# Three pairs of rounded weight tiles instead of two in a streaming-encoder block on one core

## The chip, the core and the metric

The kernel runs on one core of a Trainium2 chip. The core has a matrix engine (TensorE, PE in the profile, with its weight loads as PEld), a vector engine (DVE), a scalar engine (ACT), GpSimd (POOL) and a sync engine (SP) that here issues most DMAs. The metric is the device time of one execution in microseconds (us). The time before is the median of three runs.

## The reference

One layer of a hybrid encoder block on 256 tokens of width 2048, all in float32, and the result must be close to float32. Four sublayers follow each other, each ending in a layer norm over the residual stream:

```python
h = LN(alpha*h + 0.5*swiglu(h, ffn1))            # 2048 -> 2 x 5504 -> 2048
proj = h @ w_in                                   # q/k/v of A, latents of B, two gates
y_a = chunked_attention(q, k, v, rel_bias) @ w_o_a     # 16 heads of 64
y_b = latent_attention(q_lat, kv_lat, ...) @ w_o_b     # 16 heads, rotary part of 64
h = LN(alpha*h + (sig(g_a)*y_a + sig(g_b)*y_b) @ w_out)
h = LN(alpha*h + cross_attention(h, LN(mem)))     # 4 heads of 512, 256 memory tokens
h = LN(alpha*h + 0.5*swiglu(h, ffn2))
```

About 480 MB of weights are read once. Each weight meets all 256 tokens.

## The kernel before

**Split operands.** A float32 product is made of three faster products. Each operand is rounded to a shorter format (float32r), hi, and what the rounding leaves out, lo, is kept as a second operand of that format; hi·hi, hi·lo and lo·hi are added in PSUM. For weights this is done by `halves` (lines 257 to 266): two casts on ACT of 128x1024 each (line 262) write hi, then one subtraction on DVE (line 265) writes lo. Activations go the same way through `split` (lines 253 and 254).

**Weights as a queue.** The block's work is a list of items. An item is a function that issues matmuls and the weight pieces it needs, 1 MB each, 128x2048 elements. `run` (lines 177 to 242) walks the list. Before an item's function is called, it loads its pieces and, as far as `ahead` allows, those of later items: `fetch` starts the DMA on SP into one of three raw tiles, `halves` issues the roundings into a pair of tiles from `unit` (pools whi and wlo, `UNITS` each). What limits the look-ahead is the last line:

```python
def ahead(need, held):
    if nxt < need:
        return True
    n = sum(not early(w) for w in queue[need:nxt])
    return (nxt < need + 5 and (early(queue[nxt]) or n < 2)
            and held + live + slots(queue[nxt]) <= UNITS)
```

`live` counts pieces loaded but not used up, `held` the pairs that an item keeps for a later one. With `UNITS` at 2 there is the piece in use and one more.

**Two sorts of step.** In `pair_group` (lines 643 to 667) a group makes two output blocks for both halves of the tokens from eight steps of two k-tiles each. A plain step (`mm_pair`, line 309) takes 24 matmuls. At steps 2, 4 and 6 a scheme of the Strassen kind (`mm_sums`, line 363) does with 21. It needs sums of weight blocks, made on DVE by `weight_sums` (lines 246 and 248) in a stage tile (H5 in most groups, a raw tile in others), rounded by `halves` into X2 (hi) and X3 (lo), which have one buffer each. It also needs sums of activations (`sum_forms`, lines 319 to 328), some of which stay in four tiles of 128x256 from `w1` for all groups of a stage. After step 6, `shared` (lines 674 to 679) takes four PSUM banks out; these are the banks in which the next group begins, half a dozen matmuls after step 7.

**Other users of the small tiles.** `total` (lines 279 to 288) adds two halves of a PSUM tile through a `w1` tile; the attention heads' queries and keys stay there until their scores are made.

**Order.** The program is written in the order of the items, but a scheduler orders each engine's instructions by priority (`prio`) and by its own estimate of when each can run, and picks free tiles of a pool. Each engine then works in that order and waits at the first instruction that isn't ready. Transposes of activations are DMAs on SP, issued behind the last weight load (`issue_after`), so loads and transposes share one ordered queue. POOL issues a few loads of biases, norm vectors, memory tokens and rotary swaps; their descriptors are written into a scratch of the SBUF whose size the program's builder sets (`kernel`, line 1761).

Of the kernel before, what the change touches and what calls it, by code (L numbers as in the profile page):

```python
# [47 lines left out]
RMS_EPS = 1e-6  # L48
NEG = -1e30
MAGIC = 0x5F3759DF  # L50
UNITS = 2
SOON, NEAR, LATE = 400, 100, -400
WARM = 9
HEADS = ("H4", "H5", "X2", "X3")
# [45 lines left out]
class Kernel:  # L100
    def __init__(self, ctx, tc, t, out):
        self.tc, self.nc, self.t, self.out = tc, tc.nc, t, out

        def pool(name, bufs=1, **kw):
            return ctx.enter_context(tc.tile_pool(name=name, bufs=bufs, **kw))

        self.const = pool("const")
        self.wraw = pool("wraw", 3)
        self.whi = pool("whi", UNITS)
        self.wlo = pool("wlo", UNITS)  # L110
        self.blocks = pool("blocks")
# [22 lines left out]
        return self.work.tile(list(shape), dt, tag="w2", bufs=6, name=self.name("w2"))  # L134

    def w1(self, shape=(P, S), dt=F32):
        return self.work.tile(list(shape), dt, tag="w1", bufs=6, name=self.name("w1"))

    def sm(self, tag, n, dt=F32, bufs=None):
        return self.small.tile([P, n], dt, tag=tag, name=self.name(tag), **({"bufs": bufs} if bufs else {}))  # L140
# [36 lines left out]
    def run(self):  # L177
# [3 lines left out]
        def slots(w):  # L181
            return 0 if isinstance(w, tuple) and w[1] else 1
# [35 lines left out]
        def early(w):  # L218
            return not isinstance(w, Sums) and w[1] is not None and "early" in w[1]
# [8 lines that stand above are left out]
# [1543 lines left out]
```

## Time and profile before

| | us |
|---|---|
| median of three runs | 2436.41 |
| lowest, highest | 2433.37, 2439.05 |
| span of the profiled execution | 2432.9 |
| PE busy in the span | 2423.0 |
| DVE busy | 2121.1 |
| ACT busy | 1551.3 |

The span reaches from the first to the last instruction of one execution. For the profiled execution itself the page gives no time beside this span, so the three timed runs, 0.5 to 6.2 us longer, show what lies around it. In the rows, "mm" and "at" are PSUM tiles, "hi" and "lo" a weight pair, "T", "H" and "X" blocks of activations or, where line 262 or 265 writes X from H, rounded weight sums. A row of the timeline has its start, its length, the engine, the line and the operation, the tiles and the count of merged instructions, and in brackets the engine's idle time before it and what ended it.

### The profile page before, as it was taken

How to read it: one execution, taken by the hardware profiler on the slowest of the kernel's cores; microseconds unless marked ns; L12 is line 12 of the kernel's file. 1: busy time of each engine (PE TensorE's matmuls, PEld its weight loads, DVE VectorE, ACT ScalarE, POOL GpSimd, SP SyncE). 2: the span in 40 equal slices, each digit the busy share in tenths (PEclk: the TensorE clock that was granted, in tenths of full speed). 3: DMA queues.
4: the chain of work that ended last, by engine and by line, in shares of the span. 5: the costliest groups of instructions: out<-in, count | busy, mean ns of one | idle time of the engine just before them, and what ended most of it. 6: DMA issues, size and time to landing. Idle time of an engine off the chain costs nothing.

```text
span 2432.9 us, 29701 instructions
## 1 busy us (share of the span) xinstructions
PE 2423.0 (100%) x11286; PEld 2022.5 (83%) x11286; DVE 2121.1 (87%) x2423; ACT 1551.3 (64%) x2017; POOL 36.1 (1%) x81
## 2 busy tenths in 40 slices
PE   9999999999999999999999999999999999999999
PEld 8888888889888888888888888888888888888887
DVE  8999989899878898789788889979879999888997
ACT  6676745666555557878565687765666675556762
POOL 0000000000000001000000000000000000000000
PEclk9999999999999999999999999999999999999999
DMA  7766656666645657776577577655556666666665
GB/s 268 252 214 213 208 199 221 212 199 222 225 172 209 208 209 248 230 209 175 184 249 251 167 236 218 219 184 189 190 199 214 229 221 210 216 208 205 201 223 182
DMA packets 176414, 516.20 MB, mean 212 GB/s; under 512 B 111728, under 2 KB 112496, under 8 KB 121104
## 3 DMA queue, kind: packets, MB, share of 16 engines
q1 hardware_dynamic: 170816, 495.83, 61.2%
q0 software_dynamic: 4592, 17.30, 2.2%
q8 instruction: 88, 1.44, 0.2%
q10 hardware_dynamic: 864, 1.18, 0.1%
q14 instruction: 54, 0.44, 0.1%
HBM read 485.30 MB, written 2.10 MB: 200 GB/s over the span
## 4 chain that ended last, share of the span: by engine, by line
PE 90%; DVE 4%; ACT 3%; DMA 1%; issue 1%; SPq 0%; DVEq 0%; ACTq 0%
PE at L309 24%; PE mm L309 23%; PE mm L296 11%; PE at L363 10%; PE mm L363 10%; PE mm L275 5%; PE mm L277 2%; DVE lo L265 2%; ACT hi L262 1%; PE at L1028 1%; DMA raw<-w_xq 0%; PE at L1499 0%; PE at L1082 0%; PE at L275 0%; DMA raw<-w_o_b 0%
## 5 line engine op out<-in xcount | busy, mean ns | idle before, releaser
L262 ACT CAST hi<-raw 128x1024 fp32r<-128x1024 f32 (+1 forms) x852 | 805.3, 982 | 454.2 <-PE at L309 155.0
L265 DVE TENSOR_TENSOR lo<-raw,hi 128x2048 fp32r<-128x2048 f32 (+1 forms) x427 | 902.3, 2114 | 139.3 <-ACT hi L262 133.4
L309 PE MATMUL mm<-hi,T 128*128 128x512 f32 (+1 forms) x1328 | 311.1, 384 | 1.3 <-DVE v L397 1.3
L309 PEld LDWEIGHTS mm<-hi,T 128*128 128x128 f32 x1328 | 247.3, 188 | 48.5 <-DVE v L397 1.8
L309 PE MATMUL at<-hi,T 128*128 128x512 f32 x1152 | 275.5, 389 | 0.0
L262 ACT CAST X<-H 128x1024 fp32r<-128x1024 f32 (+1 forms) x166 | 170.6, 1034 | 162.0 <-DVE H L246 128.1
L309 PEld LDWEIGHTS at<-hi,T 128*128 128x128 f32 x1152 | 216.2, 188 | 45.1
L265 DVE TENSOR_TENSOR X<-H,X 128x2048 fp32r<-128x2048 f32 (+1 forms) x83 | 186.7, 2250 | 68.6 <-ACT X L262 68.6
L309 PE MATMUL mm<-lo,T 128*128 128x512 f32 (+1 forms) x664 | 160.4, 382 | 0.0
L309 PEld LDWEIGHTS mm<-lo,T 128*128 128x128 f32 x664 | 123.7, 188 | 22.8
L309 PE MATMUL at<-lo,T 128*128 128x512 f32 x576 | 142.4, 389 | 0.0
L309 PE MATMUL at<-hi,H 128*128 128x512 f32 x560 | 133.7, 389 | 0.0
L309 PEld LDWEIGHTS at<-lo,T 128*128 128x128 f32 x576 | 108.1, 188 | 22.5
L309 PEld LDWEIGHTS at<-hi,H 128*128 128x128 f32 x560 | 104.9, 188 | 21.6
L309 PE MATMUL mm<-hi,H 128*128 128x512 f32 x480 | 115.5, 391 | 0.3 <-DVE w L679 0.3
L248 DVE TENSOR_TENSOR H<-H,raw 128x512 f32<-128x512 f32 (+1 forms) x166 | 112.2, 676 | 2.2
L309 PEld LDWEIGHTS mm<-hi,H 128*128 128x128 f32 x480 | 89.5, 188 | 19.3 <-DVE w L679 0.8
L246 DVE TENSOR_TENSOR H<-raw 128x1024 f32<-128x1024 f32 (+1 forms) x83 | 99.4, 1198 | 0.9 <-DMA raw<-w_gate 0.8
L363 PE MATMUL mm<-X,X 128*128 128x512 f32 x342 | 91.1, 392 | 0.0
L262 ACT CAST X<-raw 128x1024 fp32r<-128x1024 f32 (+1 forms) x54 | 55.4, 1036 | 48.7 <-DVE raw L248 38.7
L363 PE MATMUL at<-X,X 128*128 128x512 f32 (+1 forms) x315 | 82.5, 386 | 0.9 <-DVE X L265 0.5
L849 ACT COPY w<-w 128x1024 uint16<-128x1024 uint16 (+1 forms) x60 | 75.8, 1276 | 0.6 <-DMA w<-w 0.5
(373 smaller groups left out, 4123.1 us busy)
## 6 DMA issues: line engine op xcount, KB each, us to landing
raw<-ffn_w_in SPq DMA_DIRECT2D x150, 1024.0 KB, 4.8
raw<-ffn_w_out SPq DMA_DIRECT2D x66, 1024.0 KB, 4.8
raw<-w_gate SPq DMA_DIRECT2D x32, 1024.0 KB, 4.8
raw<-ffn_w_out_r SPq DMA_DIRECT2D x16, 1024.0 KB, 4.9
raw<-w_qk SPq DMA_DIRECT2D x16, 1024.0 KB, 5.5
raw<-w_o_b SPq DMA_DIRECT2D x16, 1024.0 KB, 4.8
raw<-w_out SPq DMA_DIRECT2D x16, 1024.0 KB, 5.2
raw<-w_xk SPq DMA_DIRECT2D x16, 1024.0 KB, 5.3
```

The source lines that it names most:

```text
L246: self.nc.vector.tensor_tensor(two[0], two[1], raw[:, :m].unsqueeze(1).to_broadcast([P, 2, m]), ALU.add)
L248: self.nc.vector.tensor_tensor(t[:, a * m:a * m + m], t[:, b * m:b * m + m], raw[:, a * m:a * m + m], ALU.add)
L262: self.last_hi = self.nc.scalar.copy(hi[:, c:d], src[:, c:d])
L265: self.last_lo = self.nc.vector.tensor_tensor(lo[:, :n], src, hi[:, :n].bitcast(F32), ALU.subtract)
L275: self.nc.tensor.matmul(ps, hi[j], x.both(kt), start=(j == 0), stop=False)
L277: self.last_mm = self.nc.tensor.matmul(ps[:, :S], lo[j], x.at(0, kt), start=False, stop=(j == n - 1))
L296: self.last_mm = self.nc.tensor.matmul(ps, x.at(xi, kt)[:, tt * P:(tt + 1) * P], w[wi][:, j * 512 + c:j * 512 + c + m], start=(start and j ...
L309: self.last_mm = self.nc.tensor.matmul(ps[tt, g][:, :n], x.at(xi, kt)[:, tt * P:(tt + 1) * P], w[wi][:, c:c + n], start=first and j + wi + ...
L363: self.last_mm = self.nc.tensor.matmul(bank[:, :m], a[xi], v[wi][:, c * m:(c + 1) * m], start=own and first and wi + xi == 0, stop=own and ...
L849: self.nc.scalar.copy(self.words(u, n).rearrange("p (c k) -> p k c", k=2), self.words(s, n).rearrange("p (k c) -> p k c", k=2))
L1028: nc.tensor.matmul(ps[:, c0:c0 + nk], q[:, tt * P:(tt + 1) * P], k[:, :nk], start=(j == 0), stop=(j == len(parts) - 1))
```

## The change

The diff, whole:

```diff
-UNITS = 2
+UNITS = 3
 SOON, NEAR, LATE = 400, 100, -400
...
     def w1(self, shape=(P, S), dt=F32):
-        return self.work.tile(list(shape), dt, tag="w1", bufs=6, name=self.name("w1"))
+        return self.work.tile(list(shape), dt, tag="w1", bufs=4, name=self.name("w1"))
...
-    nc = bacc.Bacc("TRN2", target_bir_lowering=False, num_devices=1)
+    nc = bacc.Bacc("TRN2", target_bir_lowering=False, num_devices=1, dynamic_dma_scratch_size=2048)
```

There is a third tile of 8 KB per partition for hi and one for lo. Two small tiles of 1 KB each go, and the scratch for descriptors of POOL's DMAs is set to 2 KB. `ahead` now lets one more piece be loaded and rounded before an item, so its roundings are issued one weight earlier; what is computed stays. The program has the same instructions on every engine. Of PE's 11107 matmuls 514 stand at another place, of ACT's 1949 and DVE's 2425 instructions some 700 each, POOL's order is the same, and of SP's 580 some 40 stand elsewhere.

Two places show how. The first is the end of a gate group (the third `pair_group` of w_gate). On DVE, L265 lo is the rounding of a plain weight (lo_6070 before and lo_6046 after are the same weight, that of step 7), L265 X_908 is the rounding of the sums of step 6, L246 and L248 build sums in H5, and L676 to L679 are `shared`. Before:

```order
L248 TENSOR_TENSOR H_904_6008<-H_904_6008,raw_6006 128x512 x2
L265 TENSOR_TENSOR X_908_6039<-H_904_6008,X_907_6038 128x2048
L265 TENSOR_TENSOR lo_6070<-raw_6067,hi_6069 128x2048
L676 TENSOR_TENSOR w_917_6104<-w_915_6102,mm_5942 128x512
L265 TENSOR_TENSOR lo_6098<-raw_6095,hi_6097 128x2048
L677 TENSOR_TENSOR w_916_6103<-w_916_6103,w_917_6104 128x512
L678 TENSOR_TENSOR w_917_6104<-w_917_6104,mm_5943 128x512
L679 TENSOR_TENSOR w_918_6105<-w_916_6103,mm_5943 128x512
```

And now, in the same place on DVE:

```order
L248 TENSOR_TENSOR H_904_5984<-H_904_5984,raw_5982 128x512
L265 TENSOR_TENSOR lo_6046<-raw_6043,hi_6045 128x2048
L265 TENSOR_TENSOR X_908_6018<-H_904_5984,X_907_6017 128x2048
L265 TENSOR_TENSOR lo_6077<-raw_6074,hi_6076 128x2048
L246 TENSOR_TENSOR H_923_6121<-raw_6119 128x1024
L248 TENSOR_TENSOR H_923_6121<-H_923_6121,raw_6119 128x512
L265 TENSOR_TENSOR lo_6115<-raw_6112,hi_6114 128x2048
L676 TENSOR_TENSOR w_917_6104<-w_915_6102,mm_5952 128x512
L248 TENSOR_TENSOR H_923_6121<-H_923_6121,raw_6119 128x512
L677 TENSOR_TENSOR w_916_6103<-w_916_6103,w_917_6104 128x512
L678 TENSOR_TENSOR w_917_6104<-w_917_6104,mm_5953 128x512
L679 TENSOR_TENSOR w_918_6105<-w_916_6103,mm_5953 128x512
```

The lo of step 7 moved from behind X to ahead of it, and ahead of L676 there are now both lo of the next group's first two steps and most of the sums for its step 2. On ACT at the same place (X_907 is the hi of the sums, L674 and L675 are the copies of `shared`), before:

```order
L262 CAST X_907_6038<-H_904_6008 128x1024
L262 CAST hi_6069<-raw_6067 128x1024
L262 CAST X_907_6038<-H_904_6008 128x1024
L262 CAST hi_6069<-raw_6067 128x1024
L262 CAST hi_6097<-raw_6095 128x1024
L674 COPY w_915_6102<-mm_5940 128x512
L262 CAST hi_6097<-raw_6095 128x1024
L675 COPY w_916_6103<-mm_5941 128x512
```

and now:

```order
L262 CAST hi_6045<-raw_6043 128x1024 x2
L262 CAST X_907_6017<-H_904_5984 128x1024 x2
L262 CAST hi_6076<-raw_6074 128x1024 x2
L262 CAST hi_6114<-raw_6112 128x1024
L674 COPY w_915_6102<-mm_5950 128x512
L262 CAST hi_6114<-raw_6112 128x1024
L262 CAST X_927_6164<-H_923_6121 128x1024
L675 COPY w_916_6103<-mm_5951 128x512
```

Both casts of step 7's weight stand ahead of X's, and the casts of the next group's second weight and one of its step 2 sums stand ahead of L675. The second place is in the second query group of the cross attention, on DVE, where L323 and L254 make a form of activations (w, then T) for the sums step that reads it. Before:

```order
L248 TENSOR_TENSOR T_1892_12194<-T_1892_12194,raw_12192 128x512
L323 TENSOR_TENSOR w_1894_12201<-w_1893_12200,w_1894_12201 128x128
L323 TENSOR_TENSOR w_1894_12201<-w_1893_12200 128x128
L265 TENSOR_TENSOR lo_12231<-raw_12192,hi_12230 128x1536
L254 TENSOR_TENSOR T_1877_12114<-w_1894_12201,T_1877_12114 128x512
L265 TENSOR_TENSOR X_1898_12236<-T_1892_12194,X_1897_12235 128x2048
```

and now:

```order
L265 TENSOR_TENSOR lo_12164<-raw_12161,hi_12163 128x2048
L265 TENSOR_TENSOR X_1883_12130<-T_1876_12086,X_1882_12129 128x2048
L254 TENSOR_TENSOR T_1877_12114<-w_1894_12201,T_1877_12114 128x512
L246 TENSOR_TENSOR T_1892_12170<-raw_12168 128x1024
L265 TENSOR_TENSOR lo_12210<-raw_12168,hi_12209 128x1536
L248 TENSOR_TENSOR T_1892_12170<-T_1892_12170,raw_12168 128x512
```

The form's last row (L254, T_1877) moved ahead of the same step's L246 and lo (lo_12231 before, lo_12210 now).

## The prediction

> **What bounds the kernel now.** I read the page's head and the chain that ended last first, to see which engine carries the time.
>
> ```profile
> span 2432.9 us, 29701 instructions
> ...
> PE 2423.0 (100%) x11286; PEld 2022.5 (83%) x11286; DVE 2121.1 (87%) x2423; ACT 1551.3 (64%) x2017; POOL 36.1 (1%) x81
> ...
> PE 90%; DVE 4%; ACT 3%; DMA 1%; issue 1%; SPq 0%; DVEq 0%; ACTq 0%
> ```
>
> TensorE is busy for 2423.0 of 2432.9 us. A busy matmul row can hide a wait, because 0.39 us long matmuls overlap, so I counted matmuls in stretches of the span (columns: stretch, its length, then busy us and count of PE, PEld, DVE, ACT, POOL, then the granted clock and the DMA share).
>
> ```profile
> 200.00:300.00 100.00, 100.00 (x442) 82.59 (x441) 93.66 (x89) 69.28 (x79) 0.00 (x0) 1.00 0.63 202
> ...
> 1900.00:2000.00 100.00, 100.00 (x442) 82.47 (x441) 96.06 (x95) 69.41 (x80) 3.22 (x6) 1.00 0.67 218
> 2000.00:2100.00 100.00, 99.47 (x439) 82.00 (x438) 90.46 (x83) 58.48 (x65) 0.00 (x0) 1.00 0.60 204
> ```
>
> The granted clock is 1.00. 442 matmuls in 100 us are one per 0.227 us, and this pace is the same in distant stretches; where it stalls, some are missing (439: three matmuls, 0.7 us). So nearly all of the time is matmuls at their own pace, and the change, which leaves all 11107 matmuls of the program as they are, can only work on stalls. What they are is best read from the waits of PEld, the weight loads, since those don't overlap (us in total, times, longest).
>
> ```profile
> PEld mm L363 <- DVE X L265: 2.2, 8, 0.3
> PEld at L363 <- DVE X L265: 2.1, 5, 1.0
> PEld mm L309 <- DVE v L397: 1.8, 1, 1.8
> PEld at L363 <- ACT X L262: 1.5, 4, 0.5
> ...
> PEld mm L309 <- DVE w L679: 0.9, 2, 0.8
> PEld at L1082 <- ACT T L849: 0.9, 2, 0.6
> PEld mm L363 <- DVE T L254: 0.8, 1, 0.8
> ...
> PEld mm L363 <- DVE H L254: 0.7, 2, 0.3
> ...
> PEld at L1082 <- ACT H L849: 0.4, 1, 0.4
> PEld mm L275 <- ACT hi L262: 0.4, 1, 0.4
> ```
>
> Only the last row is a weight pair that came late, which is what the change gives a third of. The largest sum, 5.8 us in 17 stalls, is X: the rounded sums of weights (X2, X3), which have one buffer before and after, but are made by the same DVE and ACT queues. One such stall, in the gate groups:
>
> ```profile
> 827.83 1.29 PE L309 MATMUL mm<-hi,T 128*128 128x512 f32 x5
> 828.99 0.96 PE L363 MATMUL at<-X,X 128*128 128x512 f32 x3
> 829.79 0.40 PE L363 MATMUL mm<-X,T 128*128 128x512 f32 x1
> ...
> 828.99 0.53 PEld L363 LDWEIGHTS at<-X,X 128*128 128x128 f32 x3 [0.29 <-DVE X L265]
> ...
> 824.44 2.29 DVE L265 TENSOR_TENSOR lo<-raw,hi 128x2048 fp32r<-128x2048 f32 x1 [0.74 <-ACT hi L262]
> 826.65 2.28 DVE L265 TENSOR_TENSOR X<-H,X 128x2048 fp32r<-128x2048 f32 x1
> ```
>
> From 827.83 to 829.79 eight matmuls start in 1.96 us where 8 x 0.227 = 1.81 would do: 0.15 us are lost, 0.14 less than PEld's 0.29. I take 0.14 off each stall of the waits. X ended at 828.93 because DVE did a pair's lo (2.29 us) before it, and waited 0.74 us for ACT before that.
>
> **The change, part by part. The third pair.** The steady state of a group shows what it does. A plain step (24 matmuls) and a sums step (21) take turns, 45 x 0.227 = 10.20 us for both.
>
> ```profile
> 797.46 3.79 PE L309 MATMUL at<-hi,T 128*128 128x512 f32 x16
> 801.09 1.98 PE L309 MATMUL at<-lo,T 128*128 128x512 f32 x8
> ...
> 804.26 0.39 PE L363 MATMUL at<-lo,T 128*128 128x512 f32 x1
> ...
> 806.75 0.84 PE L363 MATMUL mm<-X,w 128*128 128x512 f32 x3
> ...
> 807.66 3.79 PE L309 MATMUL at<-hi,T 128*128 128x512 f32 x16
> ...
> 797.57 1.22 DVE L246 TENSOR_TENSOR H<-raw 128x1024 f32<-128x1024 f32 x1
> ...
> 800.38 1.41 DVE L248 TENSOR_TENSOR H<-H,raw 128x512 f32<-128x512 f32 x2
> 803.36 2.29 DVE L265 TENSOR_TENSOR X<-H,X 128x2048 fp32r<-128x2048 f32 x1 [1.58 <-ACT X L262]
> 805.57 2.28 DVE L265 TENSOR_TENSOR lo<-raw,hi 128x2048 fp32r<-128x2048 f32 x1
> ...
> 801.33 1.05 ACT L262 CAST hi<-raw 128x1024 fp32r<-128x1024 f32 x1 [1.37 <-PE at L309]
> ```
>
> Before: the cast for the plain step of 807.66 waits until 801.33 for the hi tile of the step of 797.46. It stands among the casts of X, so X starts at 803.36 after 1.58 us of idle DVE and ends at 805.65, 1.10 us before PE needs it at 806.75. After: this cast needs the tile of the sums step one earlier, free at 804.26 - 10.20 = 794.06. Counting on with these durations in the new order: hi 794.1 to 796.1 (two casts), the plain lo 796.1 to 798.4, the X2 casts 796.55 (X2's release, 806.75 - 10.20) to 798.6, X 798.7 to 801.0. **The slack grows from 1.1 to 5.8 us, although a lo is now ahead of X.** In the new order a lo stands so ahead of X at 49 of its 106 uses, and 32 of these had no more slack than this 1.1. In steady state this costs nothing, covered by DVE being one weight ahead. Where it isn't, each costs 2.28 - 1.10 = 1.18 and the restart's 0.15 - 0.03: 1.3 us.
>
> The loads move with it: raw of that weight is free at 798.4 instead of 807.85, and its next load starts then on SP's queue. The transposes behind it wait no longer than before, since the load they follow leaves earlier.
>
> ```profile
> raw<-w_gate SPq DMA_DIRECT2D x32, 1024.0 KB, 4.8
> ```
>
> It lands at 803.2, before its first reader below. With a DMA share of 0.6 to 0.7 there is room.
>
> **At the ends of groups** the first sums of the next group and two lo now stand ahead of L676 to L679, which free the PSUM banks for the next group.
>
> ```profile
> 811.89 0.68 DVE L679 TENSOR_TENSOR w<-w,mm 128x512 f32<-128x512 f32 x1
> ...
> 813.10 1.07 PE L309 MATMUL mm<-hi,T 128*128 128x512 f32 x4
> ```
>
> The fourth bank is asked for at 813.10 + 6 x 0.227 = 814.46; L679 ended at 812.57, slack 1.9. After, lo (its tile is free at 801.09 + 8 x 0.227 = 802.90, its hi at 803.1) 803.1 to 805.4, L246 to 806.6, L248 to 807.3, lo to 809.6, then L676, L248, L677, L678, L679 at 0.69 each: 813.1. The slack is 1.4 us: nothing, but a load that lands over 3 us late would be seen there.
>
> **What of the stalls goes.** X: 5.8 - 17 x 0.14 = 3.4; the longest (1.0, in out_pair, 0.86 net) stands with the same rows around it, so 2.5 go. The pair's own hi: 0.4. T by L254: 0.8 - 0.14 = 0.66, its row now ahead of the lo that held it. The 1.8 (L397) is the mixer's turn, where DVE's rows are the same: stays. L849: 1.3 with its sister in H, unclear, between -1.0 and +1.0, I take 0. L679: 0.9 - 0.28 = 0.6 in all; at its 0.8 a lo of 2.28 now comes first, against 1.24 us in which DVE waited for ACT, so between -0.6 and +1.0: 0.
>
> **The small tiles and the scratch.** Four w1 bind most where eight totals follow each other with two tiles held.
>
> ```profile
> 1046.44 1.09 PE L275 MATMUL mm<-X,hi 128*128 128x512 f32 x4
> ...
> 1047.85 1.09 PE L275 MATMUL mm<-X,hi 128*128 128x512 f32 x4
> ...
> 1050.67 0.64 ACT L283 COPY w<-mm 128x256 f32<-128x256 f32 x2
> 1053.01 1.13 DVE L284 TENSOR_TENSOR T<-w,mm 128x256 f32<-128x256 f32 x3
> ...
> T<-T POOLq DMA_DIRECT2D x4, 128.0 KB, 5.2
> ```
>
> A copy can wait 2.35 us for the add two before it. PE makes such a tile in 1.41 us (1046.44 to 1047.85) and has four banks, so 3 x 1.41 = 4.2 us are covered: 0, at most 8 x 2.35 = 19 with that cover gone. The smaller scratch touches POOL's queue alone. If each of its loads waited for the one before, the four swaps of T would take 4 x 5.2 = 21 us; they serve heads 8 to 15, which come after seven other heads: 0, at most 21. Both upper ends lie in what the range leaves out. The Trainium skill (SBUF — State Buffer, section on the SBUF's size) names 16 KiB as what these descriptors' rings take; no row here shows a ring fill.
>
> **Sum.** 2432.9 - 2.5 - 0.4 - 0.66 = 2429.3 for the span. The three timed runs lie 0.5 to 6.2 above the span shown, their median 3.5: **2432.8 us**, 0.15% below 2436.41. A measurement of this kernel tells about 0.2% (4.9 us) from no change.
>
> **Rivals.**
> 1. *All stalls near roundings go*: 5.8 - 2.4 of X, 0.4, 0.66, L679 0.6, L849 0.9, H by L254 0.4: 6.4 us, 2430.0. For it: slack is five times what it was. Against it: PSUM, LN and joins aren't waits for a pair. The Trainium skill (Perfetto Trace Analysis, Optimization Strategy) says that the same gap repeating can mean too few buffers; here the gap repeats, but behind X, whose buffers stay at one. It also calls matmul busy time a poor measure and points to LDWEIGHTS (83%); by that an estimated 17%, some 410 us, would be open, which the even 0.227 us contradicts. Chance 0.2.
> 2. *Slower: X behind the lo.* If DVE doesn't get 1.18 us ahead, all 32 steps lose 1.3: 42 us, 2475. For it: DVE is at 94% in the first feed-forward's groups (200 to 300) and at 96% between 1900 and 2000, where little is left to get ahead with. Lost there alone, it is nine steps, 12 us: 2445 with the gain kept elsewhere. Against it: PE, not DVE, sets the pace, so the lead has time to build. It decides at a lead of 1.18 us. Chance 0.17.
> 3. *The pairs aren't used deeper* (loads or sums' raw tiles hold the queue): 2436. Chance 0.08.
>
> The forecast itself has 0.55. **Range:** rival 1 less 1.5 of run-to-run spread, 2428.5, to rival 2's partial case with the same spread, 2447. Faster by over 0.2% (below 2431.5) holds rival 1 and a part of the forecast's lower side: 0.25; within 0.2%: 0.58; slower: 0.17.
>
> **What would show it.** Right: DVE's X ends 4 to 6 us ahead of its matmuls in the groups' middles, the X rows of PEld's waits fall from 5.8 to under 2.5, L397's 1.8 stays, ACT's waits for PE at L309 shorten because casts run earlier. Wrong: L309 waiting for L679 at more than two group ends, X rows longer than 1 us in many steps, or rows of lo or hi among PEld's waits. What would make the number wrong is a stage in which loads or DVE don't keep the lead, which the steady state can't show.

## The result: 1.4% slower, and the profile after

The changed kernel takes **2468.79 us** (median of 4 runs, 2467.0 to 2469.92) against 2436.32 us before (2433.37 to 2439.05): ratio 1.0137, 95% interval [1.0123, 1.0151]. The forecast of 2432.8 us, its range (up to 2447) and its sign are all wrong.

First the page of the changed kernel: the head, and the chain of work that ended last.

```profile
span 2468.1 us, 29651 instructions
...
PE 2431.7 (99%) x11286; PEld 2028.6 (82%) x11286; DVE 2120.3 (86%) x2423; ACT 1546.3 (63%) x2017; POOL 35.9 (1%) x81
...
PE 72%; DVE 10%; ACT 8%; DMA 5%; issue 4%; SPq 0%; DVEq 0%; ACTq 0%
```

The work is the same: as many matmuls and DVE instructions, and DVE is busy for 2120.3 us against 2121.1. But DVE and ACT now have 18% of the chain against 7%. The 35.2 us more of span split in two: time without a matmul is 2468.1 - 2431.7 = 36.4 us against 9.9 (26.5 more), and the same 11286 matmuls are busy for 8.7 us more. Most of the second part is matmuls at a lower clock (an estimated 7.7 us, worked out in the last section); waits hidden in a matmul's row can be the rest.

The waits of PEld (us in total, times, longest) name what TensorE stood for.

```profile
PEld mm L309 <- DVE w L679: 10.4, 8, 3.1
PEld mm L275 <- DVE w L284: 8.1, 2, 7.5
PEld at L363 <- ACT X L262: 5.5, 5, 1.4
PEld at L309 <- DVE w L679: 4.4, 5, 1.9
PEld mm L309 <- DVE w L284: 2.9, 1, 2.9
...
PEld at L363 <- DVE X L265: 0.8, 3, 0.3
PEld mm L363 <- DVE X L265: 0.7, 1, 0.7
```

One part of the wait that the change was forecast to shorten did shorten: X by DVE (L265) from 4.3 to 1.5 us. New are 14.8 us for L679, the last evacuation of a group end (0.9 before), and 11 us for L284, the totals (0.3 before in the same kind of row); X by ACT's casts rose from 1.5 to 5.5, so that X's rows together rose, from 5.8 to 7.0.

**A group end.** The same place in the two traces, DVE and TensorE, before and then after. A row is start, duration, and what the work is; idle time ahead of it stands in brackets.

```profile
1499.67 0.69 DVE L676 TENSOR_TENSOR w<-w,mm 128x512 f32<-128x512 f32 x1 [0.33 <-ACT w L674]
1501.60 2.29 DVE L265 TENSOR_TENSOR lo<-raw,hi 128x2048 fp32r<-128x2048 f32 x1 [1.24 <-ACT hi L262]
1503.81 0.69 DVE L677 TENSOR_TENSOR w<-w,w 128x512 f32<-128x512 f32 x1
1504.53 0.69 DVE L678 TENSOR_TENSOR w<-w,mm 128x512 f32<-128x512 f32 x1
1505.14 0.68 DVE L679 TENSOR_TENSOR w<-w,mm 128x512 f32<-128x512 f32 x1
...
1498.58 3.79 PE L309 MATMUL at<-hi,T 128*128 128x512 f32 x16
...
1505.87 2.57 PE L309 MATMUL mm<-hi,H 128*128 128x512 f32 x10 [0.33 <-DVE w L679]
```

```profile
1521.69 2.29 DVE L265 TENSOR_TENSOR lo<-raw,hi 128x2048 fp32r<-128x2048 f32 x1 [1.73 <-ACT hi L262]
1523.90 0.68 DVE L676 TENSOR_TENSOR w<-w,mm 128x512 f32<-128x512 f32 x1
1524.69 0.69 DVE L677 TENSOR_TENSOR w<-w,w 128x512 f32<-128x512 f32 x1
1525.30 2.29 DVE L265 TENSOR_TENSOR lo<-raw,hi 128x2048 fp32r<-128x2048 f32 x1
1527.50 0.68 DVE L678 TENSOR_TENSOR w<-w,mm 128x512 f32<-128x512 f32 x1
1528.10 0.68 DVE L679 TENSOR_TENSOR w<-w,mm 128x512 f32<-128x512 f32 x1
...
1519.17 3.79 PE L309 MATMUL at<-hi,T 128*128 128x512 f32 x16
...
1528.83 3.81 PE L309 MATMUL mm<-hi,H 128*128 128x512 f32 x10 [2.70 <-DVE w L679]
```

Measured from the start of the plain step (1498.58 and 1519.17), L679 ended after 7.24 us before and ends after 9.61 us now. Two lo of 2.29 us stand ahead of it in that time, where one did, and L676 starts 4.73 us into the step instead of 1.09. The fourth bank that L679 frees is asked for as early as ever, and TensorE stands for 2.70 us. In DVE's order a lo stands between L676 and L679 at 25 of the 39 group ends, against 15 before. All 13 waits for L679 come at ends of these 25, none at the other 14.

**The attention heads.** Here it begins on ACT. First the rows before, then after: ACT, and under them TensorE.

```profile
1034.43 1.56 ACT L841 COPY w<-w 128x768 uint16<-128x768 uint16 x2
1035.90 0.36 ACT L283 COPY w<-mm 128x256 f32<-128x256 f32 x1
1036.16 1.05 ACT L262 CAST hi<-raw 128x1024 fp32r<-128x1024 f32 x1
1038.67 2.00 ACT L262 CAST hi<-raw 128x1024 fp32r<-128x1024 f32 x2 [1.46 <-PE mm L275]
1040.57 1.05 ACT L849 COPY w<-w 128x768 uint16<-128x768 uint16 x1
...
1032.90 2.08 PE L277 MATMUL mm<-T,lo 128*128 128x256 f32 x16
```

```profile
1052.61 1.56 ACT L841 COPY w<-w 128x768 uint16<-128x768 uint16 x2
1054.07 0.36 ACT L283 COPY w<-mm 128x256 f32<-128x256 f32 x1
1054.34 1.05 ACT L262 CAST hi<-raw 128x1024 fp32r<-128x1024 f32 x1
1056.28 1.05 ACT L849 COPY w<-w 128x768 uint16<-128x768 uint16 x1 [0.89 <-DMA w<-w]
1057.20 1.98 ACT L262 CAST hi<-raw 128x1024 fp32r<-128x1024 f32 x2
1059.09 0.36 ACT L283 COPY w<-mm 128x256 f32<-128x256 f32 x1
...
1041.78 2.08 PE L277 MATMUL mm<-T,lo 128*128 128x256 f32 x16
...
1063.92 2.07 PE L275 MATMUL mm<-X,hi 128*128 128x512 f32 x4 [7.29 <-DVE w L284]
```

L849 (the function `join`, so the document calls these places joins) takes back the probabilities whose transposes L841 has just made possible. Before, three hi casts stand between the two, and the transposes have mostly landed when ACT comes to L849 (0.5 us of waiting for them in all, 850 to 1070 us). Now one does, and L849 waits 0.89 us for its DMA with two casts behind it. The delay goes round through DVE and back to ACT:

```profile
1059.21 2.29 DVE L265 TENSOR_TENSOR lo<-raw,hi 128x2048 fp32r<-128x2048 f32 x1 [1.50 <-ACT hi L262]
...
1063.32 0.40 ACT L827 ACTIVATE w<-w,sm_m 128x128 f32<-128x128 f32 x1 [2.42 <-DVE sm_m L825]
```

DVE's lo waits for those two casts, the row maxima of the next scores (L824, L825) stand behind that lo in DVE's queue, and ACT's exponentials (L827) wait for the maxima. Once round takes 13.4 us here (L827 starts at 1049.90 and 1063.32) and 15.1 us three heads earlier (1006.59, 1021.65), where TensorE needs 13.0 for a head (1027.45 to 1040.47 before, L1082). So head by head ACT falls behind: the copy L283 that starts a total follows its matmuls within 1 us before (32.90 + 2.08 = 34.98, copy at 35.90), but 10.2 us later now (43.86, copy at 54.07). As long as banks are free that costs nothing. Then eight totals in a row need the banks, and TensorE stands for 7.29 us.

### The profile page after: what moved, and what is told of

Read it like the earlier page. It is cut to its first block, busy times and chain, and to the rows that moved or that the text cites. A ratio compares the mean times of both kernels' runs of the same rounds, so it can differ in the third digit from the quotient of the medians.

```text
span 2468.1 us, 29651 instructions
## 1 busy us (share of the span) xinstructions
PE 2431.7 (99%) x11286; PEld 2028.6 (82%) x11286; DVE 2120.3 (86%) x2423; ACT 1546.3 (63%) x2017; POOL 35.9 (1%) x81
## 4 chain that ended last, share of the span: by engine, by line
PE 72%; DVE 10%; ACT 8%; DMA 5%; issue 4%; SPq 0%; DVEq 0%; ACTq 0%
PE mm L309 21%; PE at L309 20%; PE at L363 9%; PE mm L363 8%; PE mm L296 6%; DVE lo L265 4%; ACT hi L262 4%; PE mm L275 3%; DMA raw<-ffn_w_in 2%; PE mm L277 1%; ACT w L849 1%; PE at L1028 1%; ACT X L262 1%; DMA raw<-w_xv 1%; DMA raw<-w_va 1%
## 5 line engine op out<-in xcount | busy, mean ns | idle before, releaser
L262 ACT CAST hi<-raw 128x1024 fp32r<-128x1024 f32 (+1 forms) x852 | 804.0, 982 | 538.2 <-PE at L309 109.5
L265 DVE TENSOR_TENSOR lo<-raw,hi 128x2048 fp32r<-128x2048 f32 (+1 forms) x427 | 903.8, 2118 | 181.4 <-ACT hi L262 171.7
L309 PE MATMUL mm<-hi,T 128*128 128x512 f32 (+1 forms) x1328 | 311.4, 384 | 5.4 <-DVE w L679 3.9
L309 PEld LDWEIGHTS mm<-hi,T 128*128 128x128 f32 x1328 | 247.5, 188 | 54.1 <-DVE w L679 5.8
L309 PE MATMUL at<-hi,T 128*128 128x512 f32 x1152 | 275.2, 389 | 2.5 <-DVE w L679 2.5
L309 PEld LDWEIGHTS at<-hi,T 128*128 128x128 f32 x1152 | 215.9, 188 | 48.8 <-DVE w L679 4.0
L265 DVE TENSOR_TENSOR X<-H,X 128x2048 fp32r<-128x2048 f32 (+1 forms) x83 | 187.0, 2253 | 35.9 <-ACT X L262 35.9
L309 PE MATMUL mm<-lo,T 128*128 128x512 f32 (+1 forms) x664 | 159.7, 382 | 0.0
L309 PE MATMUL at<-lo,T 128*128 128x512 f32 x576 | 142.6, 389 | 0.0
L309 PEld LDWEIGHTS mm<-lo,T 128*128 128x128 f32 x664 | 123.6, 188 | 22.8
L309 PE MATMUL at<-hi,H 128*128 128x512 f32 x560 | 133.3, 389 | 0.0
L309 PEld LDWEIGHTS at<-lo,T 128*128 128x128 f32 x576 | 108.1, 188 | 22.4
L309 PE MATMUL mm<-hi,H 128*128 128x512 f32 x480 | 118.2, 397 | 5.8 <-DVE w L679 3.3
L309 PEld LDWEIGHTS at<-hi,H 128*128 128x128 f32 x560 | 104.9, 188 | 21.9 <-DVE w L679 0.4
L248 DVE TENSOR_TENSOR H<-H,raw 128x512 f32<-128x512 f32 (+1 forms) x166 | 113.1, 681 | 1.6
L309 PEld LDWEIGHTS mm<-hi,H 128*128 128x128 f32 x480 | 90.8, 191 | 26.1 <-DVE w L679 4.6
L246 DVE TENSOR_TENSOR H<-raw 128x1024 f32<-128x1024 f32 (+1 forms) x83 | 99.9, 1204 | 1.6 <-DMA raw<-ffn_w_in 0.9
L849 ACT COPY w<-w 128x1024 uint16<-128x1024 uint16 (+1 forms) x60 | 73.6, 1269 | 7.3 <-DMA w<-w 7.3
```

Of the source, the lines that this page charges most:

```text
L246: self.nc.vector.tensor_tensor(two[0], two[1], raw[:, :m].unsqueeze(1).to_broadcast([P, 2, m]), ALU.add)
L248: self.nc.vector.tensor_tensor(t[:, a * m:a * m + m], t[:, b * m:b * m + m], raw[:, a * m:a * m + m], ALU.add)
L262: self.last_hi = self.nc.scalar.copy(hi[:, c:d], src[:, c:d])
L265: self.last_lo = self.nc.vector.tensor_tensor(lo[:, :n], src, hi[:, :n].bitcast(F32), ALU.subtract)
L309: self.last_mm = self.nc.tensor.matmul(ps[tt, g][:, :n], x.at(xi, kt)[:, tt * P:(tt + 1) * P], w[wi][:, c:c + n], start=first and j + wi + ...
L849: self.nc.scalar.copy(self.words(u, n).rearrange("p (c k) -> p k c", k=2), self.words(s, n).rearrange("p (k c) -> p k c", k=2))
```

## The experiments

Twelve kernels were run. The kernel before took 2433.3 to 2435.2 us beside them, so each difference here is taken from its own comparison's time of before; the changed kernel's is +32.5 us (2468.79 - 2436.32).

Two theories came first. A: roundings two weights ahead stand in front of evacuations in the in-order queues of DVE and ACT. B: four w1 tiles hold up the totals. What the first runs left of A became C (two places carry the loss, the joins and the group ends) and then E (the order, and nothing else).

**Which of the three parts?** Three kernels: four w1 tiles alone; all three parts, but with the planner (`ahead`) held to one weight ahead; and five w1 tiles.

```diff
# a1_four_w1, from the kernel before
-  tag="w1", bufs=6
+  tag="w1", bufs=4
# a2_third_pair_no_lookahead, from the changed kernel
-  and held + live + slots(queue[nxt]) <= UNITS)
+  and held + live + slots(queue[nxt]) <= 2)
# a3_lookahead_five_w1, from the changed kernel
-  tag="w1", bufs=4  ...  dynamic_dma_scratch_size=2048
+  tag="w1", bufs=5  ...  dynamic_dma_scratch_size=1024
```

> The kernel before with four tiles w1 instead of six; two pairs of weight halves and the default DMA scratch stay. Theory A (the roundings two weights ahead stand in front of evacuations in the queues of DVE and ACT): nothing of the loss is here, 2434 to 2439 us, and no wait of PE for a total (L284) above 1 us. Theory B (four w1 tiles hold up the totals of the rope and query steps, which wait 8.1 us for L284 in the changed kernel, with slow matmuls behind them): 2446 to 2452 us, with a wait of several us for L284 near 1050 us and near 1600 us in this kernel too.

> The changed kernel (three pairs, four w1 tiles, 2 KB scratch), but the planner still rounds only one weight ahead (its limit written as 2), so that the third pair only spares waits for a pair to come free. Theory A (rounding two ahead costs): the loss is gone, 2430 to 2440 us, waits for L679 back under 2 us in sum. Theory B (w1 or scratch): still 2446 us or more with L284 waits of several us; a third reading, that the third pair itself or the scratch costs: 2465 us as in the changed kernel.

> The changed kernel with five w1 tiles instead of four (the room comes from a DMA scratch of 1 KB). Theory A: 2465 to 2470 us as the changed kernel, both waits (L679 about 14.8 us, L284 about 11 us) stay. Theory B: the L284 waits near 1060 and 1628 us (10 us, and about as much again in matmuls at a lower clock) go, 2450 to 2456 us, while those for L679 stay at 12 to 15 us.

a1: 2432.92 us, -0.5, ratio 0.9997 [0.9987, 1.0006]: four w1 tiles with two pairs cost nothing. a3: 2465.58 us, +32.2, ratio 1.0125 [1.011, 1.014], with the 7.5 us wait for L284 in place (and 11.6 us for L679): the small tiles are not what makes the totals late. Theory B is out.

a2 goes against both theories and came out as its third reading had it (the third pair itself or the scratch costs): 2464.4 us, +31.0, ratio 1.0123 [1.0106, 1.0139], with the same waits as the changed kernel (10.9 and 3.7 us for L679, 8.1 for L284). In DVE's order a lo stands between L676 and L679 at the same count of ends, 25. So it isn't the planner's limit either. The planner only decides where a rounding is written. Where it is queued is decided when the program is laid out, by when its operands and its buffer come free; a third pair is free sooner, and that alone moves the roundings forward past evacuations and joins. Theory A holds only in this form.

**Undo one place.** b1 puts L849 behind the newest rounding again, b2 keeps the roundings that are written behind a group end queued behind that end's evacuation, b3 does both (b2 and b3 stand on a2, whose own loss is 31.0 us), b4 gives three tiles to the high halves only.

```diff
# b1_join_behind_hi, from the changed kernel
-  with self.tc.issue_after((behind or self.next_hi).ins):
+  with self.tc.issue_after((behind or self.last_hi).ins):
# b2_group_ends_fenced, from a2; b3_both: b1 and b2
-  nc.scalar.copy(b, q[1])
+  self.hi_gate = nc.scalar.copy(b, q[1])
-  nc.vector.tensor_tensor(c, b, q[3], ALU.subtract)
+  self.gate = nc.vector.tensor_tensor(c, b, q[3], ALU.subtract)
...
+  with self.after(self.hi_gate): self.last_hi = ...
+  with self.after(self.chain), self.after(self.gate): self.last_lo = ...
# b4_three_hi_two_lo, from the kernel before (w1 as there, scratch 2 KB)
-  self.whi = pool("whi", UNITS)
+  self.whi = pool("whi", 3)
```

> The changed kernel; only the copies that take the transposed probabilities back (L849) are put behind the newest rounding on ACT, instead of the roundings of the next weight, so that in the attention heads three hi casts stand between the transposes' start (L841) and L849 again, as before, and not one. Theory C (L849 moved ahead of two casts waits for its transposes, ACT falls behind PE head by head, and PE at last waits 7.3 us for a total, L284): ACT's idle time before L849 near 970 to 1070 us falls from 7.3 us to under 1, the waits for L284 near 1060 us go, and with them the matmuls at a lower clock there: 2454 to 2459 us. Theory D (the roundings themselves delay the totals): the L284 wait stays above 5 us and the time at 2463 to 2469.

> The third-pair kernel of run a2 in which roundings that are written behind a group end may not be queued ahead of that group end's evacuation (on ACT behind L675, on DVE behind L679). Theory C (at group ends a rounding that the third pair made ready early stands between L676 and L679, so that the banks come free some 2.3 us late): the L679 waits fall from 14.6 us to under 5, the attention's L284 wait of 7.5 us stays, time 2448 to 2456 us. Rival (PE is held at group ends by something else, so that L679 is late in any order): L679 waits stay above 10 us, time above 2460.

> Both edits, the fence at group ends and L849 behind the newest rounding, with the third pair, four w1 tiles and the 2 KB scratch in place. Theory C: what is left of the loss is under 8 us, 2430 to 2441 us, since the two kinds of wait and the low clock behind them made most of it. Rival (third pair, w1 or scratch cost by themselves): above 2445.

> The kernel before with three tiles for high halves, but two for low halves, planner limit two, six w1 tiles, a DMA scratch of 2 KB. In DVE's order the roundings between L676 and L679 then are as few as before (14 groups' worth against 16; 42 in the changed kernel), while on ACT L849 stands ahead of the casts, with one cast before it, as in the changed kernel. Theory C: the L679 waits stay under 3 us and those for L284 near 1055 us appear (5 to 8 us, ACT's idle before L849 about 7 us): 2440 to 2452 us. If early low halves carry all of the loss: 2430 to 2436. If the scratch costs: above 2455.

b1: 2457.67 us, +22.4 (ratio 1.009 [1.0072, 1.0108]), 10 less than the changed kernel, as theory C expected: the wait of 7.5 us is gone, ACT's idle time ahead of L849 in the attention falls from 7.3 to 0.6 us, and the stretch of 1000 to 1100 us has 597 matmuls against 537, 10 us' worth. It isn't a clean cut, though: the layout moved elsewhere, too, and the waits for L679 fell from 14.8 to 8.4 us while X by L265 rose from 1.5 to 5.5. b2: 2460.8 us, +25.6 (1.0109 [1.0093, 1.0125]), 5.4 less than a2, a miss: the L679 waits fell to 1.5 us as expected, but a part of the loss only moved: X waits rose, as b2's waits show.

```profile
PEld mm L275 <- DVE w L284: 8.5, 2, 7.8
PEld at L363 <- ACT X L262: 7.4, 8, 2.1
PEld at L363 <- DVE X L265: 5.9, 7, 2.8
```

b3: 2449.32 us, +14.1, ratio 1.0062 [1.0046, 1.0078], 17 less than a2, above the 2441 that theory C allowed and where its rival was (buffers that cost by themselves, which c1 tests below); neither L679 (0.8 us) nor the attention's L284 is left, but 7.6 us for X by L265 are, and many small waits. The two repairs together take back over half of a2's loss, not all, and repairs of single places push others out of order. b4: 2447.92 us, ratio 1.0055 [1.0039, 1.0071], in the expected range, but not by the expected way: the waits for L679 were 4.5 us, not under 3. ACT did stand for L849 (8.3 us), while no wait for L284 over 2.2 us came and the stretch of 1000 to 1100 us lost nothing. Waiting at L849 is thus not enough by itself for the totals to stall. The traces show what differs: in b4 DVE's lo ahead of the row maxima starts at 1041.19 us, while the casts behind L849 run from 1040.91 to 1042.89, so it doesn't need them, and L827 keeps TensorE's 13.0 us a head (1032.28, 1045.30). No run changes this alone.

**Order or buffers?** The decisive test keeps the third pair, the four tiles and the small scratch, but lays the program out with two pairs first and then fixes that order, for every engine (c1), for DVE alone (c2) or for ACT alone (c3).

```diff
# c1_held_order, from a2
-  nc = bacc.Bacc(...)  ...  tile_block_kernel(tc, t, out)
+  _, order = _build(arrays, 2)
+  nc, _ = _build(arrays, 3, order)
...
+  for names in order.values():
+      for a, b in zip(names, names[1:]):
+          tc.add_manual_dep(traced[b], a, NoSync)
```

> Three pairs, four w1 tiles and the 2 KB scratch, but every engine's instructions in the order that they have with two pairs (the program is first laid out with two pairs, and that order is then fixed by order-only edges while it is laid out with three). Only what a buffer frees at run time is left of the change. Theory E (the whole loss is in the order in which ACT, DVE and PE now issue, none in the buffers, the w1 tiles or the scratch): 2428 to 2435 us, no wait for L679 or L284 above 1 us, no low clock near 1060 us. Rival (pair, tiles, scratch or addresses cost by themselves): above 2442.

> As c1, but only DVE keeps its order of two pairs; ACT, PE and the transfers are ordered anew, and on ACT the copies L849 stand behind one cast instead of three in the attention heads. If DVE's order alone carries the loss (low halves ahead of evacuations): 2430 to 2436. If ACT's order carries a part of it (L849 ahead of the casts): 2440 to 2455, with ACT idle for L849's transposes and a wait for L284 near 1055 us of several us.

> As c1, but only ACT keeps its order of two pairs. Theory E with DVE following ACT (a low half cannot be formed before its high half is cast, so holding ACT holds DVE, too): 2430 to 2437 us, waits for L679 under 4 us. If DVE's own order matters even so: 2440 or more with L679 waits above 5 us.

c1: **2427.19 us**, -6.1, ratio 0.9973 [0.9962, 0.9985], faster than both kernels. The buffers, the tiles and the scratch cost nothing together; they gain 6.1 us. So the order costs all of the 32.5 us and these 6.1: 38.6 (37.1 counted from a2, on which c1 stands). c2: 2445.2 us (1.0046 [1.0032, 1.006]) and c3: 2448.74 us (1.0062 [1.0048, 1.0075]): holding one engine's order alone isn't enough. They aren't shares of the loss, since an old order beside new ones may cost by itself. c2's time is in the range for a part in ACT's order, but the wait for L284 near 1055 us didn't come. c3's expectation of theory E was a miss, as holding ACT doesn't hold DVE; its waits for L679 were 4.1 us, under the 5 expected if DVE's order matters, and waits for hi casts (9.6 us) are its largest.

What the third pair does in either order is best seen on ACT: the casts of hi, their count, busy time and mean, then the idle time ahead of them and what ended most of it, for before, after and c1.

```profile
L262 ACT CAST hi<-raw 128x1024 fp32r<-128x1024 f32 x723 | 739.4, 1050 | 454.2 <-PE at L309 155.0 <-PE mm L309 119.8 <-PE mm L296 42.3
```

```profile
L262 ACT CAST hi<-raw 128x1024 fp32r<-128x1024 f32 x723 | 737.4, 1050 | 538.2 <-PE at L309 109.5 <-DMA raw<-ffn_w_in 90.5 <-PE mm L309 87.3
```

```profile
L262 ACT CAST hi<-raw 128x1024 fp32r<-128x1024 f32 x723 | 732.9, 1049 | 193.8 <-PE at L309 32.0 <-DMA raw<-ffn_w_out 30.6 <-PE mm L309 25.7
```

Before, ACT stands 454.2 us ahead of hi casts, mostly until TensorE has read the pair. With the order held the third pair cuts this to 193.8 us. In the changed kernel it rises to 538.2 us: the casts are queued so early that they stand at the head of ACT's queue for a pair or for weights that haven't landed (90.5 us for the load of ffn_w_in), and what is queued behind them stands, too.

**One place by itself.** d1 makes only the join's move in the kernel with two pairs, d2 only a move of the group ends' kind in c1.

```diff
# d1_two_pairs_early_join, from the kernel before, line 1072
-  rot_hi[0] if rot_hi else None
+  rot_hi[0] if rot_hi else self.now_hi
# d2_held_lo_ahead, from c1: at 29 group ends in DVE's fixed order
+  dve.remove(near[0]); dve.insert(dve.index(e), near[0])   # e: L678, near[0]: the next lo
```

> The kernel before, with two pairs, in which only the copies L849 of the attention's first heads stand earlier in ACT's queue: ahead of the two casts of the next weight in most heads (one cast between L841 and L849 instead of three); PE, DVE and POOL keep every row. Theory C (this alone makes ACT wait for the transposes and fall behind PE, until PE waits for a total): idle before L849 of 5 to 8 us, a wait of PE for L284 of 5 to 8 us near 1045 to 1055 us, slow matmuls behind it, 2440 to 2448 us. Rival (without the third pair PE does not get ahead, so nothing is lost): 2431 to 2436.

> The kernel of run c1 (three pairs, order of two), in which at 29 group ends one rounding of a low half (2.29 us on DVE) is moved ahead of L678 and L679, as in the changed kernel; ACT, PE and the transfers keep every row. If the banks' release there has the slack of 1.4 to 1.9 us that the prediction took, 0.4 to 0.9 us at an end: 12 to 26 us in all, 2438 to 2452, with waits for L679 at ten or more ends. If only the ends at which ACT is late, too, count: 2428 to 2434.

d1: 2440.85 us, +7.4, ratio 1.0032 [1.0021, 1.0042], for moved copies alone. The loop of the changed kernel is there (L827 at 1007.89, 1021.33, 1036.10 and 1049.53, 13.4 to 14.8 us a head). The wait for L284 came, but was 2.8 us and not 5 to 8; idle ahead of L849 is 4.7 us, just under the expected 5, and 2.0 us more went to a lo (L265).

```profile
1050.14 1.57 PE L275 MATMUL mm<-X,hi 128*128 128x512 f32 x4 [2.63 <-DVE w L284]
...
1052.36 1.91 PE L275 MATMUL mm<-X,hi 128*128 128x512 f32 x4
```

d2: 2440.96 us, +7.5, ratio 1.0031 [1.002, 1.0043], so 13.6 us above c1 (7.5 + 6.1), inside the expected 12 to 26. Its waits for L679 are 11.3 us at ten places; in the traces ACT, PE and POOL keep c1's order.

```profile
PEld at L309 <- DVE w L679: 7.8, 6, 2.1
PEld mm L309 <- DVE w L679: 3.5, 4, 2.3
```

So each of the two moves costs by itself, 13.6 and 7.4 us. d1's is the changed kernel's own move in the attention. d2's is of the same kind, but larger and at other ends: 44 lo between L676 and L679 at 36 ends, where the changed kernel has 27 at 25, and only two of its ten waits come at ends where the changed kernel waits. It shows that the move costs, not what it costs in the changed kernel, and the two aren't to be added up to a share of the 38.6. How that divides stays open: the group ends, X behind the casts, T and H by L254, the totals outside of the attention, and what the moves do to each other.

## Why the prediction was wrong, point by point

- **What bounds the kernel** was right in that a kernel with fewer stalls (c1) is faster. That the change can only work on stalls was not: the pace of 0.227 us went, too, where the clock fell behind a stall, an estimated 7.7 us for which the sum has no term.
- **The steady state in the groups' middle** was right at the place worked out. X was to be ready 5.8 us ahead instead of 1.1. In the changed kernel it ends at 799.99 and the matmuls that use it start at 805.66, 5.67 us ahead:

```profile
797.70 2.29 DVE L265 TENSOR_TENSOR X<-H,X 128x2048 fp32r<-128x2048 f32 x1 [0.16 <-ACT X L262]
...
805.66 0.84 PE L363 MATMUL mm<-X,X 128*128 128x512 f32 x3
```

But the sign that was to show the forecast right, X's rows falling from 5.8 to under 2.5 us, did not come: by ACT's casts they rose by 4.0, at five stalls, and the total is 7.0.

- **What of the stalls goes** was too low for what a third pair itself can do: 3.6 us were summed, c1 measured 6.1, near rival 1's 6.4. The 3.5 us put between span and time are in part that one execution's own: in the runs on record a time lies 1.7 to 2.2 us above its span.
- **The step that failed first is the ends of groups**: "The slack is 1.4 us: nothing". It was worked out at one end and carried to 39. At that end it came out, with a slack of 1.65 us (821.92 to 822.21 + 6 x 0.227 = 823.57):

```profile
821.24 0.68 DVE L679 TENSOR_TENSOR w<-w,mm 128x512 f32<-128x512 f32 x1
...
822.21 3.79 PE L309 MATMUL mm<-hi,T 128*128 128x512 f32 x16
```

There no lo stands between L676 and L679 now; at 25 other ends one or two do. The sum had L679 at 0, between -0.6 and +1.0, and the one stall that it looked at by itself (0.8 us, at 1505.87) became 3.1 (at 1528.83, above). PEld's waits for L679 went from 0.9 to 14.8 us in all, and d2 shows that such a move costs by itself. The sign that the prediction named, L309 waiting for L679 at more than two ends, came at 13.
- **The joins** were the second: L849 "unclear, between -1.0 and +1.0, I take 0". That bounded the wait of TensorE for L849 itself, and missed that ACT waits there with casts behind it, on which DVE's row maxima and then ACT's next exponentials and totals wait. The wait shows up under another name, L284: 11 us in all, 8.1 of them in the attention. With L849 put back (b1) the 10 us of the attention's stretch were gone, and d1 lost 7.4 by the move in the attention alone.
- **The small tiles and the scratch** at 0 were right (a1; c1 for both together). That the totals did stall, where the prediction had looked for the tiles' price, is no merit of it: a3 has the same stall with five tiles.
- **Rival 2**, slower with X behind the lo, had the right sign and not the mechanism: X's rows by DVE fell, as in the forecast. That its 2475 lies near the 2468.8 measured is chance.
- **Rival 3**, pairs not used deeper, is out: ACT's and DVE's orders moved everywhere.

## What to carry to other kernels

Where a scheduler lays out in-order queues, another buffer is not only room: it makes work ready earlier in the scheduler's eyes, and ready work can be queued ahead of the evacuations and joins that the bound engine will wait for. Before costing such a change by its steady state, list every place where a bank, a join or a total is released, and count what now stands ahead of it. If the room is wanted without the new order, lay out with the old number of buffers, hold that order and then add the buffer: here that turned 1.4% slower into 0.3% faster.

## What the runs showed of the hardware

A stall can cost more than its length. In the changed kernel the granted clock is 0.50 in four stretches and 1.00 in the rest from 4 us on to the last matmul; in the kernel before and in c1 there is no such stretch (columns: stretch, its length, then busy us and count of PE, granted clock, DMA share, GB/s).

```profile
574.09:577.50 3.41, 3.41 (x12) 0.50 0.85 356
1058.78:1069.02 10.24, 5.10 (x16) 0.50 0.82 294
1529.82:1533.23 3.41, 3.41 (x9) 0.50 0.46 87
1628.81:1632.22 3.41, 3.41 (x9) 0.50 0.85 340
```

TensorE works for 15.3 us in them; at half the clock half of that is lost, an estimated 7.7 of the 8.7 us that the matmuls take longer. Each stretch lasts 3.41 us or three times that, and each follows waits of TensorE: of 1.05 and 0.49 us close together (572.42, 573.89), of 7.29 (1063.92, where the clock fell during the wait), of 2.70 (1528.83) and of 2.45 (1628.06).

The matmul rows show the same. Groups of four that take 1.09 us elsewhere took 2.07 and 1.91 us behind the wait of 7.29. After the 2.70 us at 1528.83 the ten matmuls up to 1532.44 took 3.61 us where 10 x 0.227 = 2.27 would do, and eight lo matmuls 2.22 instead of 1.82 (1532.44 to 1534.66): 1.7 us lost behind a wait of 2.7. In d1 it was the same behind 2.63 us (1.57 and 1.91 for 1.09, above), with the clock at 0.66 in 1050 to 1055 us. A wait of 1.62 us (2239.04 us of the changed kernel) was followed by a clock of 1.00. What sets the limit between these was not tried.
